# Where the tiles start in SBUF: small tiles ahead of and behind the large ones, large tiles at multiples of 2048 bytes

## The chip, the cores and the metric

One core of one Trainium2 chip runs the program. The metric is device time in microseconds (us) of one execution; the kernel before takes 1871.26 us (median of 3 runs, 1870.98 to 1871.41). Less is better.

## The reference

Two layers of a hybrid block on one sequence of 512 tokens with 1024 features. Each layer normalises `x`, projects it to 11 groups of features, and runs three branches: attention over 128 selected keys per query, a gated linear recurrence, and a chunked spatial gate. The branches are gated, merged, projected back and added to `x`; then a squared-ReLU FFN of width 4096 and a gated per-layer embedding are added in the same way. Cut to its products:

```
h = rms_norm(x, g_pre_mix);  proj = h @ w_in                      # 1024 -> 6216 features
y_a, y_b, y_c = attention(...), rg_lru(...) * gelu(gr), gating(...)
merged = einsum(sigmoid(gate_logits), einsum('nbsw,nwd->nbsd', stack(y_a, y_b, y_c), w_branch))
x = x + rms_norm(merged @ w_out, g_post_mix)
f = square(relu(rms_norm(x, g_pre_ffn) @ w_ffn_up)) @ w_ffn_down
x = x + rms_norm(f, g_post_ffn)
x = x + rms_norm((p_i @ w_ple) * sigmoid(x @ w_ple_gate), g_post_ple)
```

## The kernel before, in words

Activations lie transposed in SBUF, features on the 128 partitions and the 512 tokens along the free dimension, so one tile is 128x512 fp32: 2048 bytes in each partition. Every fp32 product is made of three fp32r products: each operand is split into a rounded high part and the rest (`split`, lines 359 to 365), and `mm3` (lines 289 to 292) issues high·high, weight-low·high and weight-high·low into the same PSUM bank. `gemm` (line 294) runs over 8 slices of 128 features: 24 matmuls of 512 columns for one output tile. `gemm_halves` does the same in halves of 256 columns where a norm has to start early, `gemm_arriving` (line 348) where the right-hand tiles are still being made, `tokens` (line 585) with the roles exchanged (activation slices are the weights of the array, the weight tile streams). Attention has its own small products (lines 651, 654, 923, 937).

Weights come from HBM in chunks of 128x1024 fp32 on SP's queue into three buffers `wr`; ScalarE makes the high part `wh` (line 235) and VectorE the low part `wl` (line 236), four buffers each, three chunks ahead of their use. The order of the chunks is written out in the list `order`. Work of the other branches (indexer, attention, recurrence) is slotted between matmuls by `tick`, which counts estimated microseconds on `clk`; the estimates are constants in the code, so the order of instructions does not depend on addresses.

What sets addresses: `cp`, `wp` and `tp` are pools; a tile of a new tag gets the next free bytes of its pool, in the order in which the tags first appear, and pools follow one another. A tile's size is rounded up to 32 bytes. The first free byte of a partition is 16512 (8·2048 + 128), behind constants of the program. In the kernel before, small tiles (`rt`, `sm`, `vec`, `m8`, `cnt`, `mx` and others) appear between large ones. The tiles start here, as the program is built before the change:

```
tile (first of a family)   start   mod 2048   mod 128   mod 64
X0 .. X7                   16512        128         0        0
ident (128x128 fp32)       32896        128         0        0
ropeC, ropeS, sacc         36128       1312        32       32
xh0, xl0 .. xh7, xl7       42400       1440        32       32
R                          75936        160        32       32
M4 .. M1, B0 .. B7         78240        416        32       32
A0 .. A7                  107168        672        32       32
V0, K0, K1, V1 (8192 B)   123552        672        32       32
M2                        156576        928        32       32
M3                        158752       1056        32       32
wr, wh, wl (4096 B)       161120       1376        96       32
tmp (11 of them)          206176       1376        96       32
```

So `xh`, `xl`, `A`, `B`, `K`, `V`, `M`, `tmp`, `wh`, `wl` and `sacc`, which are all the large operands of matmuls, start 32 bytes behind a multiple of 64, and a slice of 128 columns of them (512 bytes) does too. `X`, which no matmul reads, and `ident`, which the transposes stream, start at multiples of 64. Before `xh0` a tile `lead` of 128 bytes is allocated that nothing uses (line 464).

Of the kernel before, what the change touches and what calls it, by code (L numbers as in the profile page):

```python
# [8 lines left out]
F32 = mybir.dt.float32  # L9
F32R = mybir.dt.float32r  # L10
BF16 = mybir.dt.bfloat16
I32 = mybir.dt.int32
# [5 lines left out]
S = 512  # L18
D = 1024
KT = 8  # L20
# [22 lines left out]
NVEC = 76  # L43
# [7 lines left out]
def hybrid_block_kernel(ctx, tc, xT, pT, pos, vec, bsp, freq, w_in, w_tok, w_lru, w_sp, w_br, w_out, w_up, w_dn, w_ple, w_gate, out, depth=DEPTH, dbg=None):  # L51
# [3 lines left out]
    cp = ctx.enter_context(tc.tile_pool(name="cp", bufs=1))  # L55
    wp = ctx.enter_context(tc.tile_pool(name="wp", bufs=1))
    tp = ctx.enter_context(tc.tile_pool(name="tp", bufs=1))
    pp = ctx.enter_context(tc.tile_pool(name="pp", bufs=1, space=PSUM))

    uid = [0]  # L60

    def nm(p):
        uid[0] += 1
        return f"{p}_{uid[0]}"

    def tmp(dt=F32):
        return tp.tile([128, S], dt, tag="tmp", name=nm("tmp"), bufs=NTMP)

    def small(n, tag="sm", bufs=8):
        return cp.tile([128, n], F32, tag=tag, name=nm(tag), bufs=bufs)  # L70

    def bank():
        return pp.tile([128, 512], F32, tag="ps", name=nm("ps"), bufs=8)

    def slot(tag, dt=F32, big=False):
        return cp.tile([128, 4, S] if big else [128, S], dt, tag=tag, name=nm(tag))
# [8 lines left out]
    NWB = 4  # L85
    LAG = 1
    TAIL = 3
    ATT = 13
    WARM = 120
    FIRST = [0, 1, 4]  # L90


    X = [cp.tile([128, S], F32, tag=f"X{k}", name=f"X{k}") for k in range(KT)]
    ident = cp.tile([128, 128], F32, tag="ident", name="ident")
    make_identity(nc, ident)
    warm = cp.tile([128, 1], F32, tag="warm", name="warm")
    V.memset(warm, 0.0)
    A.activation(warm, warm, AF.Square)
    ones2 = cp.tile([128, 2], F32, tag="ones2", name="ones2")
    V.memset(ones2, 1.0)  # L100
    mhalf = cp.tile([128, 4], F32, tag="mhalf", name="mhalf")
    V.memset(mhalf, -0.5)
    BIAS = [cp.tile([128, 128 * (t + 1)], BF16, tag=f"bias{t}", name=f"bias{t}") for t in range(4)]

    V.memset(BIAS[3], 1.0)
    wps = bank()
    for _ in range(WARM):
        PE.matmul(wps[:, 0:64], BIAS[3][:, 0:128], BIAS[3][:, 0:64], start=True, stop=True)


    tri = BIAS[0]
    G.memset(tri, 0.0)
    G.affine_select(out=tri, in_=tri, compare_op=ALU.is_ge, fill=NEG, base=0, pattern=[[-1, 128]], channel_multiplier=1)
    fq = cp.tile([128, 8], F32, tag="fq", name="fq")
    posi = cp.tile([128, 4], I32, tag="posi", name="posi")

    ropeC = cp.tile([128, S], F32, tag="ropeC", name="ropeC")
    ropeS = cp.tile([128, S], F32, tag="ropeS", name="ropeS")

# [133 lines left out]
    def defer(us, fn):  # L253
        later.append((clk[0] + us, uid[0], fn))
        uid[0] += 1
# [8 lines left out]
    def add_task(q, gen):  # L264
        q["wait"].append(gen)
# [17 lines left out]
    def finish(q):  # L283
        run_later(force=True)
        while q["act"] or q["wait"]:
            tick(0.3)
# [39 lines left out]

    def gemm_arriving(keys, xs, source, ranges, arrived=None, lag=LAG, tail=TAIL):


        n = len(keys)  # L330
        ws = [getw(key, 0) for key in keys[:-1]]
        pss = [bank() for _ in keys]
        last = {}
        for r in ranges:
            gen = source(r)
            for k in range(KT):
                with ordered(last):
                    next(gen)
                    todo = [(o, k) for o in range(len(ws))]
                    if len(ws) < n and k == lag:  # L340
                        ws.append(getw(keys[-1], 0))
                        todo += [(n - 1, q) for q in range(k + 1)]
                    if r is ranges[-1] and k >= KT - tail:
                        todo = [] if k < KT - 1 else [(o, q) for o in range(n) for q in range(KT - tail, KT)]
                    for i, (o, q) in enumerate(todo):
                        h3, l3 = [v.rearrange("p (k c) -> p k c", k=KT) for v in ws[o]]
                        for m in range(3):
                            PE.matmul(pss[o][:, r], (h3, l3, h3)[m][:, q], xs[q][m // 2][:, r], start=q == 0 and m == 0, stop=q == KT - 1 and m == 2)  # L348
                        if r is ranges[-1] and q == KT - 1 and o < n - 1:
                            prep()  # L350
                tick(0.65 * len(todo) * width(r) / S)
            if arrived is not None:
                arrived(r)
        while nprep[0] < nget[0] + LA:
            prep()
        return pss
# [103 lines left out]
                tick(0.1)  # L460
            return self.gens[r.start]


    cp.tile([128, 32], F32, tag="lead", name="lead")
    XS = [(slot(f"xh{k}", F32R), slot(f"xl{k}", F32R)) for k in range(KT)]

    def x_tiles(r, xs, g=None, st=None, ys=None, bc=None, gp=None, on_g=()):
# [3 lines left out]
        def updated(d):  # L471
            if ys is not None and d < KT:
                if gp is None:
                    V.tensor_mul(ys[d][:, r], ys[d][:, r], bc)
                else:
                    V.scalar_tensor_tensor(ys[d][:, r], ys[d][:, r], gp[:, d:d + 1], bc, op0=ALU.mult, op1=ALU.mult)
                (G if d in on_g else V).tensor_add(X[d][:, r], X[d][:, r], ys[d][:, r])  # L477

        updated(0)
        for d in range(KT):  # L480
            x = X[d][:, r]
            if xs is not None:
# [14 lines left out]
                    V.scalar_tensor_tensor(lo, x, g[:, d:d + 1], f32v(hi), op0=ALU.mult, op1=ALU.subtract)  # L497
            yield d

    vecs = [cp.tile([128, NVEC], F32, tag=f"vec{l}", name=f"vec{l}") for l in range(depth)]  # L500
    nc.sync.dma_start(vecs[0], vec[0])
    nc.scalar.dma_start(posi, pos)
    nc.scalar.dma_start(fq, freq)
# [9 lines left out]
    for k in range(KT):  # L513
        if k in FIRST:
            c = slice(128 * k, 128 * (FIRST + [KT])[FIRST.index(k) + 1])
            for src, raw, hi, lo in chunks:
                nc.sync.dma_start(raw[:, c], src[:, c])
        nc.sync.dma_start(X[k], xT[k])

# [8 lines left out]
    for l in range(depth):  # L528
# [19 lines left out]
        rt = st.rt  # L548
        first = gemm_arriving([("in", l, f"xr{j}") for j in range(3)], XS, norm.source if l else lambda r: gen0, HALVES if l else (FULL,), st.row(D, R), 0, TAIL if l else 1)

        def proj(name, ahead=LA):
            ps = bank()
            gemm(ps, getw(("in", l, name), ahead), XS, KT)
            return ps
# [11 lines left out]
        def rope(ps, n=128):  # L566
            t1, u = tmp(), tmp()
            V.tensor_mul(t1[:n], ps[:n], Cr[:n])
            V.stream_shuffle(u[:n], ps[:n], mask=SHUF)
            G.tensor_mul(u[:n], u[:n], Sr[:n])  # L570
            G.tensor_add(t1[:n], t1[:n], u[:n])  # L571
            return t1
# [108 lines left out]
        def select(t, sc):  # L681
# [20 lines left out]
            G.tensor_add(gt[:, :n], gt[:, :n], eq[:, :n])  # L702
            G.tensor_scalar(BIAS[t], gt[:, :n], -NEG, NEG, op0=ALU.mult, op1=ALU.add)
            yield 1.0
# [47 lines left out]
        for j in range(4):  # L752
            mx = tmp()
# [49 lines left out]
        sp8 = small(4, "sp8", 2)  # L803
        V.tensor_scalar(sp8, h, 8.0, None, op0=ALU.mult)
        nsp8 = small(4, "nsp8", 2)
# [70 lines left out]
        def gated(n, ys, first=None, ds=range(8)):  # L876
            for d in ds:
                th = first if first is not None and d == 0 else gate(n, d)
                if d % 2 == 0:
                    w = getw(("br", l, n, d // 2), ahead=1)  # L880
                branch(n, d, w, ys, th)
# [10 lines left out]
        def attention(j):  # L892
# [6 lines left out]
            def logits(t):  # L899
                n = 128 * (t + 1)  # L900
                pr = qk(q2, kk, (ql, ql), kk, slice(t * 128, (t + 1) * 128), max(n, 256))
                for s in range(2):
# [5 lines left out]

                    V.tensor_tensor_reduce(lt, pr[s][:, :n], BIAS[t], scale=-ATT_SCALE, scalar=3.0e38, op0=ALU.add, op1=ALU.min, accum_out=mx[:, 0:1])
                    A.activation(lt, lt, AF.Exp, scale=-1.0, bias=mx[:, 0:1], accum_out=mx[:, 1:2])  # L910
# [82 lines left out]
        for j in range(4):  # L993
            f = rope(proj(f"q{j}"))
# [8 lines left out]
            if j == 0:  # L1003
                finish(idxq)
            defer(ATT, lambda j=j: add_task(attq, attention(j)))
            gated(1, YB, ds=range(2 * j, 2 * j + 2))
# [113 lines left out]
        gp = small(8, "gp", 2)  # L1120
# [12 lines left out]
    for r in HALVES:  # L1133
        for d in norm.source(r):
            (nc.sync if d % 2 == 0 else nc.scalar).dma_start(out[d, :, r], X[d][:, r])

# [76 lines left out]
```

## Time and profile before

| what | value |
|---|---|
| median of 3 runs | 1871.26 us |
| the profiled execution's own time | 1871.55 us |
| its span, first to last instruction | 1869.8 us |
| TensorE matmul busy | 1825.9 us (98%), 8798 instructions |
| TensorE weight load busy | 1503.1 us (80%) |
| VectorE / ScalarE / GpSimd busy | 1158.4 (62%) / 802.4 (43%) / 365.8 us (20%) |
| DMA | 167.77 MB, mean 90 GB/s |
| mean granted TensorE clock | 0.992 of full speed |

Matmuls are pipelined: the duration in a row (0.39 us for 512 columns) overlaps the next one's. What a matmul costs in a run of them is the distance of the starts. A row of a window counts each matmul that lies in it wholly or in part, so the distance is the window's length plus one duration, over the count.

### The profile page before, as it was taken

The page shows a single profiled execution, that of the slowest core. Times are in us where ns is not written, and L with a number is a line of the kernel's source. Part 1 is how long each engine was busy: PE and PEld are TensorE (multiplying, and loading weights), DVE is VectorE, ACT ScalarE, POOL GpSimd, SP SyncE. Part 2 cuts the span into 40 slices and gives each one's busy share as a digit, 9 for nine tenths or more (in the row PEclk, how much of TensorE's full clock was granted, in tenths as well). Part 3 has the DMA queues.
Part 4 walks back from the last instruction along what each step waited for, and adds up shares of the span by engine and source line. Part 5 has one row for each costly group of instructions (what it writes and reads, how often), then busy time and mean ns, then how long its engine had stood idle before and what let it go on. Part 6 is the DMA issues. An engine that isn't in the chain of part 4 may idle for free.

```text
span 1869.8 us, 22869 instructions
## 1 busy us (share of the span) xinstructions
PE 1825.9 (98%) x8798; PEld 1503.1 (80%) x8798; DVE 1158.4 (62%) x1939; ACT 802.4 (43%) x1292; POOL 365.8 (20%) x292
## 2 busy tenths in 40 slices
PE   8999999999999999999999999999999999999997
PEld 7678777788888888888886787887888888888886
DVE  6689976666286253533686999666563852535355
ACT  5466436564453222223444572455544432222233
POOL 3513222210240000003454141222003200000033
PEclk9999999999999999999999999999999999999998
DMA  5122222222223322332212222222222223232321
GB/s 171 62 91 84 97 91 91 68 80 79 86 84 104 100 93 99 95 109 90 91 58 95 69 90 99 94 80 69 90 79 91 91 90 102 92 100 92 111 79 57
DMA packets 49679, 167.77 MB, mean 90 GB/s; under 512 B 6049, under 2 KB 8865, under 8 KB 49569
## 3 DMA queue, kind: packets, MB, share of 16 engines
q1 hardware_dynamic: 47376, 163.64, 27.0%
q10 hardware_dynamic: 2192, 2.67, 0.5%
q8 instruction: 69, 1.13, 0.3%
q14 instruction: 42, 0.34, 0.1%
HBM read 164.19 MB, written 2.10 MB: 89 GB/s over the span
## 4 chain that ended last, share of the span: by engine, by line
PE 74%; DVE 11%; POOL 6%; issue 5%; ACT 4%; DMA 0%; SPq 0%; POOLq 0%; ACTq 0%; DVEq 0%
PE ps L290 21%; PE ps L292 20%; PE ps L291 20%; PE ps L348 4%; PE ps L585 4%; DVE tmp L689 2%; DVE wl L236 2%; DVE m L687 2%; POOL tmp L570 1%; POOL tmp L571 1%; PE ps L937 1%; PE ps L654 1%; PE ps L651 1%; POOL sacc L390 1%; POOL X L477 1%
## 5 line engine op out<-in xcount | busy, mean ns | idle before, releaser
L235 ACT CAST wh<-wr 128x1024 fp32r<-128x1024 f32 x303 | 317.0, 1049 | 468.7 <-PE ps L292 382.8
L236 DVE TENSOR_TENSOR wl<-wr,wh 128x1024 fp32r<-128x1024 f32 x303 | 386.2, 1278 | 201.8 <-ACT wh L235 201.7
L290 PE MATMUL ps<-xh,wh 128*128 128x512 f32 (+1 forms) x1296 | 506.9, 391 | 0.0
L292 PE MATMUL ps<-xl,wh 128*128 128x512 f32 (+1 forms) x1296 | 498.1, 384 | 0.0
L291 PE MATMUL ps<-xh,wl 128*128 128x512 f32 (+1 forms) x1296 | 495.7, 382 | 0.8 <-DVE wl L236 0.8
L390 POOL TENSOR_TENSOR sacc<-sacc,tmp 128x256 f32<-128x256 f32 (+1 forms) x99 | 110.3, 1115 | 902.9 <-issue 590.1
L292 PEld LDWEIGHTS ps<-xl,wh 128*128 128x128 f32 x1296 | 243.4, 188 | 50.1
L290 PEld LDWEIGHTS ps<-xh,wh 128*128 128x128 f32 x1296 | 243.7, 188 | 49.4 <-issue 4.9
L291 PEld LDWEIGHTS ps<-xh,wl 128*128 128x128 f32 x1296 | 243.7, 188 | 46.9 <-DVE wl L236 1.7
L292 PE MATMUL ps<-V,wh 128*128 128x512 f32 (+1 forms) x528 | 196.8, 373 | 0.0
L290 PE MATMUL ps<-K,wh 128*128 128x512 f32 (+1 forms) x432 | 159.9, 370 | 0.0
L291 PE MATMUL ps<-K,wl 128*128 128x512 f32 (+1 forms) x432 | 157.9, 366 | 0.0
L292 PE MATMUL ps<-B,wh 128*128 128x512 f32 x336 | 131.9, 392 | 0.0
L290 PE MATMUL ps<-A,wh 128*128 128x512 f32 x320 | 126.6, 396 | 0.0
L291 PE MATMUL ps<-A,wl 128*128 128x512 f32 x320 | 124.8, 390 | 0.0
L1072 DVE TENSOR_TENSOR M<-M,ps 128x512 f32<-128x512 f32 x48 | 33.1, 689 | 143.8 <-PE ps L292 143.8
L292 PEld LDWEIGHTS ps<-V,wh 128*128 128x128 f32 x528 | 99.3, 188 | 18.5
L1060 DVE TENSOR_TENSOR tmp<-ps,R 128x512 f32<-128x512 f32 x64 | 43.8, 689 | 111.5 <-PE ps L292 111.5
L348 PE MATMUL ps<-xl,wh 128*128 128x256 f32 (+1 forms) x264 | 88.4, 335 | 7.8 <-DVE xl L497 7.2
L291 PEld LDWEIGHTS ps<-K,wl 128*128 128x128 f32 x432 | 81.2, 188 | 14.3
L290 PEld LDWEIGHTS ps<-K,wh 128*128 128x128 f32 x432 | 81.3, 188 | 13.2
L348 PE MATMUL ps<-xh,wh 128*128 128x256 f32 (+1 forms) x264 | 87.1, 330 | 0.5 <-ACT xh L487 0.5
(239 smaller groups left out, 2745.5 us busy)
## 6 DMA issues: line engine op xcount, KB each, us to landing
wr<-in_w_in_dram SPq DMA_DIRECT2D x95, 512.0 KB, 3.3
wr<-in_w_up_dram SPq DMA_DIRECT2D x64, 512.0 KB, 3.3
wr<-in_w_dn_dram SPq DMA_DIRECT2D x64, 512.0 KB, 3.3
wr<-in_w_br_dram SPq DMA_DIRECT2D x24, 512.0 KB, 3.3
wr<-in_w_tok_dram SPq DMA_DIRECT2D x16, 512.0 KB, 3.3
wr<-in_w_out_dram SPq DMA_DIRECT2D x16, 512.0 KB, 3.3
wr<-in_w_gate_dram SPq DMA_DIRECT2D x16, 512.0 KB, 3.3
X<-in_xT_dram SPq DMA_DIRECT2D x8, 256.0 KB, 5.8
```

The source lines that it names most:

```text
L235: A.copy(hi, raw)
L236: V.tensor_sub(lo, raw, f32v(hi))
L290: PE.matmul(ps, wh, xh, start=start, stop=False)
L291: PE.matmul(ps, wl, xh, start=False, stop=False)
L292: PE.matmul(ps, wh, xl, start=False, stop=stop)
L348: PE.matmul(pss[o][:, r], (h3, l3, h3)[m][:, q], xs[q][m // 2][:, r], start=q == 0 and m == 0, stop=q == KT - 1 and m == 2)
L390: G.tensor_add(sacc[:, r], sacc[:, r], self.q[r.start, r.stop])
L585: PE.matmul(ps, x, w, start=k == 0 and i == 0, stop=k == KT - 1 and i == 2)
L687: V.max(m8, (sc if r == 0 else wk)[:, :n])
L689: V.match_replace(wk[:, :n], m8, (sc if r == 0 else wk)[:, :n], -3.0e38)
L1060: V.tensor_mul(t, ps, R)
L1072: V.tensor_add(F[d], F[d], ps)
```

## The change

All allocations of small tiles are made ahead of the first large tile, in `cp` (one unused allocation of each small tag, so that its buffers lie there; `vec0`; `warm` becomes a buffer of the tag `sm`), or in a new pool `ep` behind `tp` (`ident`, `ones2`, `mhalf`, the biases, `fq`, `posi`, `vec1`). Then a tile `lead` of 256 bytes fills up to the next multiple of 2048; the old one of 128 bytes goes. The small tiles take 1344 bytes and `vec0` 320; with `lead` that is 1920, and 16512 + 1920 = 18432 = 9·2048. From there on `cp` holds only tiles of 2048 and 8192 bytes, `wp` of 4096 and `tp` of 2048. No instruction is added or removed, and no size, buffer count, order or queue is changed.

```diff
+    ep = ctx.enter_context(tc.tile_pool(name="ep", bufs=1))
     pp = ctx.enter_context(tc.tile_pool(name="pp", bufs=1, space=PSUM))
...
+    LEAD = 256
...
-    X = [cp.tile([128, S], F32, tag=f"X{k}", name=f"X{k}") for k in range(KT)]
-    ident = cp.tile([128, 128], F32, tag="ident", name="ident")
+
+    for n, tag, bufs in ((4, "sm", 8), (4, "rt", 4), (32, "wi", 2), (8, "m8", 4), (1, "cnt", 4), (4, "sp8", 2), (4, "nsp8", 2), (2, "mx", 8), (8, "gp", 2)):
+        small(n, tag, bufs)
+    vecs = [(ep if l else cp).tile([128, NVEC], F32, tag=f"vec{l}", name=f"vec{l}") for l in range(depth)]
+    ident = ep.tile([128, 128], F32, tag="ident", name="ident")
     make_identity(nc, ident)
-    warm = cp.tile([128, 1], F32, tag="warm", name="warm")
+    warm = small(1)
     V.memset(warm, 0.0)
     A.activation(warm, warm, AF.Square)
-    ones2 = cp.tile([128, 2], F32, tag="ones2", name="ones2")
+    ones2 = ep.tile([128, 2], F32, tag="ones2", name="ones2")
     V.memset(ones2, 1.0)
-    mhalf = cp.tile([128, 4], F32, tag="mhalf", name="mhalf")
+    mhalf = ep.tile([128, 4], F32, tag="mhalf", name="mhalf")
     V.memset(mhalf, -0.5)
-    BIAS = [cp.tile([128, 128 * (t + 1)], BF16, tag=f"bias{t}", name=f"bias{t}") for t in range(4)]
+    BIAS = [ep.tile([128, 128 * (t + 1)], BF16, tag=f"bias{t}", name=f"bias{t}") for t in range(4)]
...
-    fq = cp.tile([128, 8], F32, tag="fq", name="fq")
-    posi = cp.tile([128, 4], I32, tag="posi", name="posi")
-
+    fq = ep.tile([128, 8], F32, tag="fq", name="fq")
+    posi = ep.tile([128, 4], I32, tag="posi", name="posi")
+
+    cp.tile([128, LEAD // 4], F32, tag="lead", name="lead")
+    X = [cp.tile([128, S], F32, tag=f"X{k}", name=f"X{k}") for k in range(KT)]
     ropeC = cp.tile([128, S], F32, tag="ropeC", name="ropeC")
...
-
-    cp.tile([128, 32], F32, tag="lead", name="lead")
     XS = [(slot(f"xh{k}", F32R), slot(f"xl{k}", F32R)) for k in range(KT)]
...
-    vecs = [cp.tile([128, NVEC], F32, tag=f"vec{l}", name=f"vec{l}") for l in range(depth)]
     nc.sync.dma_start(vecs[0], vec[0])
```

## Rows read from the trace of the kernel before

**Rows 1.** The page: busy time by engine, and TensorE's granted clock in 40 slices.

```profile
PE 1825.9 (98%) x8798; PEld 1503.1 (80%) x8798; DVE 1158.4 (62%) x1939; ACT 802.4 (43%) x1292; POOL 365.8 (20%) x292
...
PEclk9999999999999999999999999999999999999998
```

**Rows 2.** The waits of TensorE: waiting line, releaser, total us, times, longest.

```profile
PE ps L348 <- DVE xl L497: 7.2, 9, 3.8
PE ps L651 <- DVE A L638: 7.1, 8, 1.9
PE ps L585 <- DVE wl L236: 4.1, 2, 2.1
```

**Rows 3.** Windows, TensorE alone: stretch, length, busy us (matmuls), granted clock, DMA.

```profile
600.00:860.00 260.00, 260.00 (x1137) 1.00 0.31 98
...
451.00:496.00 45.00, 45.00 (x195) 1.00 0.28 90
...
497.20:507.20 10.00, 10.00 (x87) 1.00 0.22 75
...
241.00:256.00 15.00, 15.00 (x66) 1.00 0.42 138
...
512.50:514.50 2.00, 2.00 (x20) 1.00 0.72 221
```

**Rows 4.** Timeline, TensorE: start us, duration us, line, tiles, shape, count.

```profile
660.72 0.39 PE L291 MATMUL ps<-xh,wl 128*128 128x512 f32 x1
...
662.09 0.39 PE L291 MATMUL ps<-xh,wl 128*128 128x512 f32 x1
...
451.20 0.40 PE L291 MATMUL ps<-A,wl 128*128 128x512 f32 x1
...
452.60 0.40 PE L291 MATMUL ps<-A,wl 128*128 128x512 f32 x1
...
512.55 0.28 PE L292 MATMUL ps<-V,wh 128*128 128x256 f32 x1
...
513.23 0.28 PE L292 MATMUL ps<-V,wh 128*128 128x256 f32 x1
```

**Rows 5.** Timeline, TensorE: transposes, and products with two columns.

```profile
31.94 1.03 PE L155 MATMUL ps<-ident,tmp 128*128 128x128 f32 x8
...
35.56 0.95 PE L400 MATMUL ps<-ones,sacc 128*128 128x2 f32 x8
```

**Rows 6.** Matmuls grouped by line and shape: count, busy us, mean ns, idle before.

```profile
L290 PE MATMUL ps<-xh,wh 128*128 128x512 f32 x1200 | 479.8, 400 | 0.0
...
L348 PE MATMUL ps<-xl,wh 128*128 128x256 f32 x176 | 52.4, 298 | 4.0 <-DVE xl L497 3.5
...
L155 PE MATMUL ps<-ident,tmp 128*128 128x128 f32 x8 | 1.0, 272 | 0.0
```

**Rows 7.** Casts of ScalarE grouped by line and shape, columns as in the group before.

```profile
L361 ACT CAST A<-tmp 128x512 fp32r<-128x512 f32 x32 | 19.9, 622 | 11.8 <-DVE tmp L1061 11.8
...
L485 ACT CAST xh<-X 128x512 fp32r<-128x512 f32 x16 | 9.8, 623 | 18.9 <-POOL X L477 16.3 <-DVE X L477 2.6
```

**Rows 8.** DMA issues: tiles, queue, count, size, median us to landing.

```profile
wr<-in_w_in_dram SPq DMA_DIRECT2D x95, 512.0 KB, 3.3
...
X<-in_xT_dram SPq DMA_DIRECT2D x8, 256.0 KB, 5.8
```

**Rows 9.** Windows, all engines: PE, PEld, DVE, ACT, POOL busy us (instructions), clock, DMA.

```profile
140.00:235.00 95.00, 93.09 (x412) 75.96 (x411) 93.14 (x168) 51.24 (x64) 30.61 (x22) 1.00 0.28 89
1065.00:1165.00 100.00, 96.00 (x420) 77.92 (x419) 98.09 (x177) 52.80 (x65) 30.61 (x22) 1.00 0.26 85
```

## The prediction

> **What bounds the kernel now.** I read the busy shares first: TensorE is busy 1825.9 of 1869.8 us and its clock is granted at the full 2.4 GHz level in nearly every slice [rows 1]. The reader is to see that there is almost no idle time to win. The waits of TensorE say the same: the three largest come to 18.4 us [rows 2]. An edit that adds and removes no instruction can then move the time only through what one matmul costs, so the third view is the distance of matmul starts in stretches without a wait, by windows.
>
> From 600 to 860 us, pure 512-column products: (260 + 0.39) / 1137 = 229.0 ns [rows 3]. 512 columns at 2.4 GHz are 213.3 ns, so 15.7 ns of each matmul, 6.9%, are not columns. From 451 to 496 us it is more: six starts take 452.60 - 451.20 = 1.40 us, 233.3 ns each [rows 4], and the window agrees, (45 + 0.40) / 195 = 232.8. The operands there are `A`, then `K` and `V`; the same `K` and `V` slots stream at the 229 ns pace later (their products lie inside 600 to 860 us). The token products of line 585 have 233.3 ns too: (15 + 0.40) / 66 [rows 3]. With 256 columns (106.7 ns at 2.4 GHz) two paces occur: (10 + 0.28) / 87 = 118.2 ns, and 0.68 / 6 = 113.3 ns [rows 3, 4].
>
> These paces are not arbitrary. 16 columns of fp32 are 64 bytes in a partition and take 16 / 2.4 = 6.67 ns. In that unit the paces are 233.3 = 35.0, 113.3 = 17.0, 229.0 = 34.35, 118.2 = 17.7. So 512 columns, 32 units, take 34.33 (103 units for three matmuls) or 35; 256 columns, 16 units, take 17 or 17.7. A stream that costs whole units of 64 bytes, always at least one too many, is what I would expect if operands are fetched in pieces of 64 bytes and every operand starts in the middle of one: 2048 bytes that begin 32 bytes behind a multiple of 64 touch 33 pieces, 1024 bytes touch 17. That is how all large matmul operands lie before the change, and the unit is an inference from the paces, not something a row states.
>
> **The change part by part.** Small tiles and `vec` move: no instruction, DMA or queue order changes, so their cost is zero on both sides. `warm` becomes a buffer of the ring `sm`: the eighth allocation after it has to wait for a ScalarE Square issued at the start of the program, over 30 us earlier; nothing. The unused allocations have no reader or writer to wait for.
>
> The large tiles of ScalarE and VectorE operands: a cast whose source is `X`, at a multiple of 64 before the change, takes 623 ns, and one whose source is `tmp`, 32 bytes off, takes 622 ns [rows 7]. Reading at a multiple of 64 gains nothing there. No row shows a write of either at such a place except VectorE's and GpSimd's into `X`, which compete with one another; and both engines are hidden behind TensorE, so I take 0. Weight transfers land in 3.3 us, and each is issued three chunks ahead, some 16 us at 5.5 us a chunk; faster or slower by 10% is hidden. The first load of `X` lands in 5.8 us [rows 8] and lies on the path once: within 0.5 us either way, taken as 0.
>
> The matmul operands: 6,808 matmuls have 512 columns (24 groups of the listing by shape) and 1,424 have 256 (17 groups); [rows 6] shows the largest group of each. The trace holds no fp32r matmul whose moving operand starts at a multiple of 64, so the new pace is bounded from both sides. Below: the transposes stream `ident`, which did start at a multiple of 64. Eight of them, first start to last end, take 1.03 us and one lasts 0.272 us [rows 5, 6], so seven starts take 0.758 us, 108.3 ns each: if they need two clocks for each of 128 columns, that is 106.7 + 1.6 ns, with no unit of 6.67 ns on top. At that excess, call it 2 ns, a 512-column matmul would cost 215.3 ns, 13.7 less than now. Above: 233.3 ns, the slower pace that exists already, 4.3 more than now. Between them I take the nearest to what the rows count: one unit of 64 bytes fewer, the same hand-over behind it, so 33.33 units, 222.2 ns, 6.7 less.
>
> Sum: 6,808 x 6.67 ns = 45.4 us. For 256 columns one unit less would be 111 ns, but there the weight load is the next limit: eight products of only two columns take 0.95 us to the last end with 0.24 for one, 0.1 us each [rows 5], and 113.3 ns is the best pace seen. So 1,424 x (118.2 - 113.3) = 7.0 us at most; many of these stand in stretches that wait for a norm (the group with 176 has a mean of 298 ns against a streaming duration of 280), and I take half, 3.5. What is late next: in two stretches VectorE is busy 93.1 of 95 and 98.1 of 100 us [rows 9]. There the 412 + 420 matmuls can't go faster than VectorE's work lets them; I take their 832 x 6.67 = 5.5 us as lost to new waits. Elsewhere VectorE and ScalarE have a third of their time or more to spare. Together 45.4 + 3.5 - 5.5 = 43.4 us. Span 1869.8 - 43.4 = 1826.4; 1.75 us lie around the span in the profiled execution (1871.55), which stands 0.3 us above the median of the runs: 1826.4 + 1.75 - 0.3 = 1828 us.
>
> [...]
>
> **The rivals.** (a) *The whole excess goes.* If the straddled start delays every piece of the stream rather than adding one, a matmul falls to 215.3 ns. For: the excess grows with the columns (6.6 or 11.5 ns at 256, 15.7 or 20 at 512), and a fixed extra piece would not. Against: 512 columns never run at 33 units now, so part of the excess is something else. Time: 6,808 x 13.7 = 93.3, plus 3.5, less 832 x 13.7 = 11.4 in VectorE's stretches: -85.4, 1786 us.
>
> (b) *Nothing changes.* The excess is the stream's own: 17/16 of 213.3 is 226.7 and of 106.7 is 113.3, and both numbers are there; fp32r would simply run 17 clocks for 16 columns wherever it starts. For: proportional excess, and ScalarE's indifference to the start [rows 7]. Against: the transposes show none. Time 1871 us. That the change does not do what it says falls here too, but 16512 + 1920 is 9·2048, and every later size is a multiple of 2048, so I give it nothing.
>
> (c) *Slower.* The pace of 35 units takes over everywhere. It lasts for 45 us at a time with operands that stream at 34.33 elsewhere, so it is a way of locking and not a property of one tile; and in the token products, where the moving operand is `wh` (96 bytes behind a multiple of 128) and the array's weights come from `xh` (32 behind), it is always there. Which lock is reached seems to hang on how the moving stream and the weight load stand to one another, and with every tile at the same phase they start in the same place each time. It decides once the 34.33 pace is no longer reached after a wait. 384 token products and some 390 in the two slow stretches pay it already: (6,808 - 774) x 4.3 ns = 26 us, 1897 us.
>
> **How the numbers follow.** Forecast 0.35, (a) 0.22, (b) 0.25, (c) 0.18. A change of 0.2%, 3.7 us, is about what these runs can tell from none. Forecast and (a) are faster: 0.57; (b) the same: 0.25; (c) slower: 0.18. The forecast's own range is 1815 to 1845 (the 256-column and VectorE terms both ways, and 33 to 34 units); (a) reaches down to 1775; on the other side the range takes in (b) with its neighbours up to 1885 and leaves most of (c) out.
>
> **What would show it.** In a stretch like 600 to 860 us: 222 ns if the forecast is right, 215 for (a), 229 for (b), 233.3 for (c); the paces in units of 6.67 ns would show whether one piece went. VectorE's and ScalarE's casts should keep 622 ns, the transposes about 108 ns. The stretches with VectorE at 95% or more should show new waits of TensorE on VectorE. The prediction is wrong if the 512-column pace stays within 1 ns of 229.0, or if it falls and the span does not follow because waits grow by as much.

## The result, and the profile after

The changed kernel takes 1861.01 us (median of 4 runs, 1858.04 to 1864.48); the kernel before takes 1871.34 us beside it (4 runs, 1870.98 to 1872.86). The ratio is 0.9942, 95% interval 0.9925 to 0.9959: about 10 us faster, where the prediction said 43. The profiled execution of the changed kernel has a span of 1857.0 us (1858.77 us with what lies around it), 12.8 us less than the span before.

The page after: span, busy time by engine and TensorE's granted clock, answering to [rows 1].

```profile
span 1857.0 us, 22869 instructions
...
PE 1812.3 (98%) x8798; PEld 1502.8 (81%) x8798; DVE 1158.3 (62%) x1939; ACT 801.9 (43%) x1292; POOL 365.0 (20%) x292
...
PEclk9999999999999999999999999999999999999999
```

TensorE's busy time falls by 13.6 us with the same 8,798 instructions and a granted clock of 0.993 after 0.992; no other engine changes by 1 us. The waits of TensorE after (columns as in [rows 2]; the lines have moved, L348 is L355, L651 is L655, L585 is L589 and L291 is L298) come to 36 us in all where they came to 35; those on `wl` grow, the one on L298 from the 3.8 us of L291, a line of before shown last:

```profile
PE ps L355 <- DVE xl L502: 7.1, 9, 3.8
PE ps L655 <- DVE A L642: 6.7, 10, 1.2
PE ps L589 <- DVE wl L243: 5.0, 2, 2.5
PE ps L298 <- DVE wl L243: 4.6, 4, 1.7
...
PE ps L291 <- DVE wl L236: 3.8, 4, 1.5
```

So the time went where the prediction looked for it, into the distance of matmul starts. Windows after, TensorE alone, columns as in [rows 3]; the second is the stretch of `A`, `K` and `V` that stood at 451 to 496 us before:

```profile
600.00:860.00 260.00, 260.00 (x1149) 1.00 0.29 99
...
449.00:494.00 45.00, 45.00 (x201) 1.00 0.29 94
...
241.00:256.00 15.00, 15.00 (x68) 1.00 0.38 125
```

From 600 to 860 us (260 + 0.39) / 1149 = 226.6 ns against 229.0. In the `A`, `K`, `V` stretch (45 + 0.40) / 201 = 225.9 against 232.8 (a little too low, for the last three of the 201 have 256 columns), in a window of nearly all token products (15 + 0.40) / 68 = 226.5 against 233.3. Single starts show a sharper value. The timeline after, TensorE, columns as in [rows 4], two rows of each of three stretches:

```profile
450.45 0.39 PE L298 MATMUL ps<-A,wl 128*128 128x512 f32 x1
...
451.81 0.39 PE L298 MATMUL ps<-A,wl 128*128 128x512 f32 x1
...
500.33 0.28 PE L298 MATMUL ps<-K,wl 128*128 128x256 f32 x1
...
501.77 0.28 PE L298 MATMUL ps<-K,wl 128*128 128x256 f32 x1
...
655.07 0.39 PE L298 MATMUL ps<-xh,wl 128*128 128x512 f32 x1
...
656.43 0.39 PE L298 MATMUL ps<-xh,wl 128*128 128x512 f32 x1
```

Six starts of 512 columns take 1.36 us in both places, 226.7 ns: 34.0 units of 6.67 ns. Twelve starts of 256 columns take 1.44 us, 120.0 ns: 18.0 units, *more* than the 113.3 to 118.2 ns before [rows 3, 4]. The 256 columns between the two cost 106.7 ns, 0.417 ns each. That is the 2.4 columns a nanosecond which the prediction writes as 2.4 GHz, and on it rest its unit of 6.67 ns, 16 columns, and its 213.3 ns for 512.

Over the whole trace, taking each start and the next of the same width, and of these distances the ones of 180 to 240 ns at 512 columns and 90 to 130 at 256 (longer ones are waits, first starts after a wait or after other products, or the lower clock): 6,407 distances at 512 columns had a mean of 229.56 ns before and have 227.29 after (6,405 of them), 1,141 at 256 columns had 116.83 and have 119.57 (1,152). 6,407 x 2.27 = 14.5 us gained, 1,141 x 2.74 = 3.1 us lost, 11.4 us together, of the span's 12.8. The mean lies above 226.7 because of the first products after a start, which vary as in the bursts of experiment 5: after the change the first ten distances of each unbroken row of them have a mean of 229.96 ns (1,218 of them), the rest 226.67 (5,187).

The two stretches with a busy VectorE, all engines, columns as in [rows 9]:

```profile
140.00:235.00 95.00, 92.70 (x409) 76.14 (x408) 93.14 (x169) 51.03 (x63) 30.56 (x22) 1.00 0.27 89
1065.00:1165.00 100.00, 95.24 (x418) 77.86 (x418) 97.97 (x179) 51.51 (x66) 27.95 (x20) 1.00 0.29 95
```

VectorE is as busy as before, and nearly as many matmuls fit in. Taking the same matmul in both traces, its start comes 1.22 us earlier after than before at 140 us and 1.66 us at 235; 7.15 us at 1065 and 7.33 us at 1165: these stretches gain 0.44 and 0.18 us. From 600 to 860 us the lead grows from 3.70 to 6.22 us.

Casts of ScalarE, one transpose group of TensorE, and the loads after (columns as in [rows 7], [rows 5] and [rows 8]):

```profile
L368 ACT CAST A<-tmp 128x512 fp32r<-128x512 f32 x32 | 19.9, 623 | 11.9 <-DVE tmp L1065 11.9
...
L490 ACT CAST xh<-X 128x512 fp32r<-128x512 f32 x16 | 9.8, 624 | 18.9 <-POOL X L482 16.3 <-DVE X L482 2.6
```

```profile
31.04 1.04 PE L162 MATMUL ps<-ident,tmp 128*128 128x128 f32 x8
```

```profile
wr<-in_w_in_dram SPq DMA_DIRECT2D x95, 512.0 KB, 3.3
...
X<-in_xT_dram SPq DMA_DIRECT2D x8, 256.0 KB, 5.7
```

All as before within 1 ns, 0.01 us and 0.1 us: these casts, transposes and transfers took as long at the new starts.

### The profile page after: what moved, and what is told of

Its sections match the earlier page's. It is cut to its first block, busy times and chain, and to the rows that moved or that the text cites. A ratio compares the mean times of both kernels' runs of the same rounds, so it can differ in the third digit from the quotient of the medians.

```text
span 1857.0 us, 22869 instructions
## 1 busy us (share of the span) xinstructions
PE 1812.3 (98%) x8798; PEld 1502.8 (81%) x8798; DVE 1158.3 (62%) x1939; ACT 801.9 (43%) x1292; POOL 365.0 (20%) x292
## 4 chain that ended last, share of the span: by engine, by line
PE 73%; DVE 12%; POOL 6%; issue 4%; ACT 4%; DMA 0%; SPq 0%; POOLq 0%; ACTq 0%; DVEq 0%
PE ps L297 21%; PE ps L299 20%; PE ps L298 20%; PE ps L355 3%; PE ps L589 3%; DVE tmp L693 2%; DVE wl L243 2%; DVE m L691 2%; POOL tmp L574 1%; POOL tmp L575 1%; PE ps L941 1%; PE ps L658 1%; POOL sacc L397 1%; POOL X L482 1%; PE ps L655 1%
## 5 line engine op out<-in xcount | busy, mean ns | idle before, releaser
L298 PE MATMUL ps<-xh,wl 128*128 128x512 f32 (+1 forms) x1296 | 495.0, 382 | 1.2 <-DVE wl L243 1.2
L298 PEld LDWEIGHTS ps<-xh,wl 128*128 128x128 f32 x1296 | 244.1, 188 | 44.4 <-DVE wl L243 2.0
L298 PE MATMUL ps<-K,wl 128*128 128x512 f32 (+1 forms) x432 | 157.8, 365 | 0.0
L298 PE MATMUL ps<-A,wl 128*128 128x512 f32 x320 | 124.5, 389 | 0.0
L355 PE MATMUL ps<-xl,wh 128*128 128x256 f32 (+1 forms) x264 | 87.9, 333 | 7.8 <-DVE xl L502 7.1
L298 PEld LDWEIGHTS ps<-K,wl 128*128 128x128 f32 x432 | 81.5, 189 | 13.1
L355 PE MATMUL ps<-xh,wh 128*128 128x256 f32 (+1 forms) x264 | 86.2, 327 | 1.2 <-ACT xh L492 1.2
```

The source lines that it names most:

```text
L298: PE.matmul(ps, wl, xh, start=False, stop=False)
```

## The experiments

What was open: is it the start of each operand (at a multiple of 64, or of 2048), is it the small tiles, or is it how two operands stand to one another? For the last, call the *difference* the start of the weights (the operand loaded into the array) less the start of the moving operand, in bytes of the partition. Starts modulo 2048 before: `xh` and `xl` 1440, `A`, `K`, `V` 672, `B` and `M` 416, `wr`, `wh`, `wl` and `tmp` 1376. After: all 0.

**1. Operands at a multiple of 64 in the kernel before.**

```diff
-    cp.tile([128, 32], F32, tag="lead", name="lead")
+    cp.tile([128, 40], F32, tag="lead", name="lead")
```

> The kernel before with its unused tile ahead of xh0 made 160 bytes instead of 128: every matmul operand from xh0 on moves from 32 to 0 modulo 64, and the tiles stay at mixed places modulo 2048 (xh at 1472, M and B at 448, A, K and V at 704, weights and tmp at 1408). Theory 64 (only the place within 64 bytes counts): the paces of the changed kernel, 226.7 ns at 512 columns and 120.0 at 256, and 1860 us. Theory 2048 (a tile must not cross a multiple of 2048): 229 and 233 ns as before, 1871 us. Theory phase (all tiles must stand alike): moving and weight tiles differ by 64 bytes modulo 128 as before, so 229 ns and 1871 us.

Measured: 1871.29 us (12 runs, 1868.76 to 1873.57), ratio 1.0007, interval 0.9998 to 1.0015. Windows, TensorE alone:

```profile
600.00:860.00 260.00, 260.00 (x1138) 1.00 0.30 99
...
241.00:256.00 15.00, 15.00 (x66) 1.00 0.32 103
```

1138 matmuls against 1137 before, 66 token products against 66. Every operand starts at a multiple of 64 and nothing has changed: the prediction's cause, a straddled piece of 64 bytes, falls. All starts moved together, so the differences are those of before.

**2. and 3. The changed kernel with its large tiles off the multiple of 2048, by 32 and by 64 bytes.**

```diff
-    LEAD = 256
+    LEAD = 32
```

That is run 2, with all large tiles at 1824 modulo 2048; run 3 has `LEAD = 64`, with all at 1856.

> The changed kernel with a filler of 32 bytes instead of 256: every large tile lies at 1824 modulo 2048, which is 32 modulo 64, and all stand alike. Theory 64: the gain is gone, paces 229 and 233 ns at 512 columns and 117.8 at 256, 1871 us. Theory phase: the paces of the changed kernel stay, 226.7 and 120.0 ns, 1861 us. Theory 2048: gone, 1871 us.

> The changed kernel with a filler of 64 bytes: every large tile lies at 1856 modulo 2048, which is 64 modulo 128 and 0 modulo 64, all alike. Theory 64 and theory phase: 226.7 and 120.0 ns, 1861 us. Theory 2048 (or any unit above 64 bytes): 229 ns or more, 1871 us.

Measured: 1859.59 us (6 runs), ratio 0.9945, interval 0.9933 to 0.9957; and 1862.88 us (5 runs), ratio 0.9961, interval 0.9949 to 0.9973. Both keep the changed kernel's paces (means of 227.3 ns at 512 and 119.6 at 256 columns). The window of run 2:

```profile
600.00:860.00 260.00, 260.00 (x1149) 1.00 0.30 99
```

1149 matmuls with tiles 32 bytes off a multiple of 64, as many as with tiles at multiples of 2048. The multiple is not what counts; that all tiles stand alike may be.

**4. The changed kernel with the weights alone 32 bytes on.**

```diff
     XS = [(slot(f"xh{k}", F32R), slot(f"xl{k}", F32R)) for k in range(KT)]
+    wp.tile([128, 8], F32, tag="wlead", name="wlead")
```

> The changed kernel with 32 unused bytes ahead of the weight pool: wr, wh, wl and tmp lie at 32 modulo 2048, the activations stay at multiples of 2048. In gemm the array's weights are off and the moving operand is not; in the token products it is the other way round. Theory 64 for the moving operand alone: 226.7 ns in gemm, 233 ns in the token products (384 matmuls, 2.5 us), 1863 us. If the weight load's place counts: 229 ns in gemm, 1871 us.

Measured: 1891.03 us (4 runs, 1889.74 to 1891.33), ratio 1.0111, interval 1.0098 to 1.0124. One unused tile of 32 bytes makes the kernel 30 us slower than the changed one. The page's busy time, and the window:

```profile
PE 1849.0 (98%) x8798; PEld 1502.7 (80%) x8798; DVE 1158.0 (61%) x1939; ACT 803.0 (43%) x1292; POOL 364.8 (19%) x292
```

```profile
600.00:860.00 260.00, 260.00 (x1116) 1.00 0.30 97
```

(260 + 0.40) / 1116 = 233.3 ns: 35 units at 512 columns, now throughout (the mean over the trace is 233.23). The moving operands are where the changed kernel has them. In run 2 both operands were 32 bytes off and the gain stayed; here the weights alone are, and it turns into a loss. So it is the relation between the two operands. Neither theory of the expectation named this time: they had 1863 and 1871 us.

**5. The difference by itself: a probe.** It leaves the kernel's computation out; its core is

```python
for i in range(48):                       # one burst, no wait inside; the bursts follow one another
    k, m = i // 3 % 8, i % 3              # hi x hi, lo weights x hi, hi weights x lo, over 8 slices
    PE.matmul(ps[:, :n], st[:, w:w + 128], mv[:, x:x + n], ...)   # w - x set by the difference
```

> A probe, not the block: it leaves out the whole computation and runs bursts of 48 matmuls, 24 in gemm's order twice, on fp32r data that nothing else touches. The moving operand starts at a multiple of 512 bytes, the weights of the array d bytes behind one, d from 0 to 512 (and 4, 8, 16, 48), three bursts of each d at 512 columns, two at 256. Then both are shifted by 32, then the moving operand alone by 32 and 64, then bfloat16. Theory phase modulo 128: 34.0 units of 6.67 ns (226.7 ns) at d = 0, 128, 256, 384, 512; 34.33 or 35 at 64, 192, 320, 448; 35 at 32, 96 and the like; shifting both by 32 changes nothing. Rival, the relation counts over a larger span: d = 128 or 256 differ from d = 0. Rival, traffic of the other engines makes the excess: without it all d have one pace, under 34 units. At 256 columns: 18.0 units at d = 0, 17.67 at 64, 17.7 at 32. bfloat16 at 512 columns, half the bytes: within 4 ns of 213.3 ns if the excess comes from the bytes that the two streams fetch.

The timeline of the probe, TensorE, one row per burst of 48: start us, us from its first start to its last end, tile names, shape. In the first fence, 512 columns, the differences are 0, 32, 64, 192 and 256 from the top, and the last row has bfloat16 operands; in the second, 256 columns, 0 and 64. In brackets stands the idle time before the burst. Each of the three probes was executed once.

```profile
38.01 11.20 PE L75 MATMUL ps<-mv,st 128*128 128x512 f32 x48 [0.73 <-ACT res L76]
49.94 11.47 PE L75 MATMUL ps<-mv,st 128*128 128x512 f32 x48 [0.73 <-ACT res L76]
62.14 11.47 PE L75 MATMUL ps<-mv,st 128*128 128x512 f32 x48 [0.73 <-ACT res L76]
...
110.93 11.26 PE L75 MATMUL ps<-mv,st 128*128 128x512 f32 x48 [0.73 <-ACT res L76]
...
135.10 11.20 PE L75 MATMUL ps<-mv,st 128*128 128x512 f32 x48 [0.73 <-ACT res L76]
...
1045.74 10.52 PE L92 MATMUL ps<-b 128*128 128x512 bf16 x47 [0.73 <-ACT res L76]
```

```profile
692.32 6.00 PE L75 MATMUL ps<-mv,st 128*128 128x256 f32 x48 [0.73 <-ACT res L76]
...
705.31 5.93 PE L75 MATMUL ps<-mv,st 128*128 128x256 f32 x48 [0.52 <-ACT res L76]
```

A burst of 512 columns starts slowly (its first distance is 333 to 344 ns, and the next ten or so can vary) and then settles on a pace that repeats within 0.1 ns in every repetition in this probe. The mean of the last 24 distances of each burst, ns:

```
difference      0     4     8    16    32    64    96   128   160   192   224   256   288   320   384   448   512
512 columns 226.7 232.3 230.7 233.3 233.3 233.3 234.3 232.7 233.3 228.9 233.3 226.7 233.3 233.3 232.1 228.9 226.7
256 columns 120.0 118.3 115.5 118.3 118.3 117.8 118.6 118.8 120.0 117.8 117.8 120.0 118.3 117.8 118.5 113.3 120.0
```

At 512 columns the pace repeats with 256 bytes but for 0.6 ns at 128 and 384. The expectation's theory, a repeat with 128 bytes, falls (128 is 6 ns slower than 0), and so does its rival that traffic of other engines makes the excess: there is next to none here (a DMA share of 0.00 or 0.01 in the windows of this probe, and one ScalarE copy between bursts). At 256 columns 192 and 448 gave 117.8 and 113.3 here, and 117.8 both in the second probe, where other bursts went before: the difference alone does not fix the pace of a burst; whether it also hangs on how the burst starts was not shown. With both operands moved by 32 bytes, difference 0 still gives 226.7 ns, and 32 and 64 still give 233.3; with the moving operand alone moved by 32 and 64 bytes, which is a difference of 224 and 192 modulo 256, the paces are 233.3 and 228.9 as in the table. Now the kernels can be read off. Before, the weights stand -64, 704 or 960 bytes behind `xh`, `A` and `B`: 192 modulo 256 each time, 228.9 ns; in the token products, with the roles exchanged, 64: 233.3 ns. Run 1 has the same differences. The changed kernel and runs 2 and 3 have 0 everywhere: 226.7 and 120.0. Run 4 has 32: 233.3 and 118.3.

**6. The whole gain from 64 bytes in the kernel before.** No small tile and no activation moves; only `wr`, `wh`, `wl` and `tmp` do.

```diff
     XS = [(slot(f"xh{k}", F32R), slot(f"xl{k}", F32R)) for k in range(KT)]
+    wp.tile([128, 16], F32, tag="wlead", name="wlead")
```

> The kernel before with one unused tile of 64 bytes ahead of the weight slots: small tiles, vec, ident and all activation slots stay where they were; only wr, wh, wl and tmp move up by 64 bytes. The weights then start 0, 768 or 1024 bytes behind the moving operands, that is 0 modulo 256, while no large tile lies at a multiple of 64. Theory (the pace hangs on the difference of the weights' start and the moving operand's start, modulo 256, and on nothing else of the change): 512 columns at 226.7 ns, 256 columns at 120 ns, token products 226.7 ns, and the whole gain of the change, 1860 to 1863 us. Rival (the multiple of 2048, or the place of the small tiles, carries part of the gain): 1866 us or more. Rival of the prediction (a start at a multiple of 64 bytes is what counts): 1871 us.

Measured: 1862.11 us (5 runs, 1860.42 to 1864.05), ratio 0.9944, interval 0.9931 to 0.9958: the same as the change. Windows, TensorE alone:

```profile
600.00:860.00 260.00, 260.00 (x1149) 1.00 0.30 98
...
241.00:256.00 15.00, 15.00 (x68) 1.00 0.38 126
```

1149 and 68, the counts of the changed kernel. The theory gave 1860 to 1863 us.

**7. The whole change but for the difference.**

```diff
-    LEAD = 256
+    LEAD = 64
...
+    wp.tile([128, 48], F32, tag="wlead", name="wlead")
```

> The kernel after with a leading tile of 64 bytes instead of 256 and an unused tile of 192 bytes ahead of the weight slots: every matmul operand starts at a multiple of 64, weights at multiples of 2048 and activations 192 bytes lower modulo 256. Theory (difference modulo 256): the paces of the kernel before, 228.9 ns at 512 columns, 233.3 ns in the token products (difference 64 there), about 117.8 ns at 256 columns; 1869 to 1873 us. Rivals (alignment to 64 or 2048, or the moved small tiles, count): at or near 1861 us.

Measured: 1872.29 us (11 runs, 1869.47 to 1873.71), ratio 1.0000, interval 0.9991 to 1.0009. The window:

```profile
600.00:860.00 260.00, 260.00 (x1137) 1.00 0.30 98
```

1137, the count of before; its mean distances (229.51 ns at 512 columns, 117.22 at 256, 233.3 in the token products) are those of before too. With the small tiles moved and the large ones at multiples of 64, but the weights 192 on, nothing is left of the gain.

**8. A difference of 256.**

```diff
-    LEAD = 256
+    LEAD = 32
...
+    wp.tile([128, 64], F32, tag="wlead", name="wlead")
```

> The kernel after with a leading tile of 32 bytes and an unused tile of 256 bytes ahead of the weight slots: activations at 1824, weights at 32 modulo 2048, difference 256. Theory (modulo 256): as the changed kernel, 226.7 and 120 ns, 1859 to 1864 us. Rival (operands must start alike modulo 2048): another pace, and 1870 us or more.

Measured: 1862.12 us (5 runs), ratio 0.9941, interval 0.9929 to 0.9954, with 1148 matmuls from 600 to 860 us. Operands that start alike modulo 256, and not modulo 2048, have the whole gain.

**9. Where the excess comes from: fewer weight columns, and alternating differences.** A second probe, again without the kernel's computation.

> Probe; the kernel's computation is left out. Bursts of 48 products that follow one another without a wait, with new weights in each product. Part 1: weights start 0, 448, 464, 480, 496, 504, 508, 192, 208, 240, 248, 64 bytes behind the moving operand, at 512 and 256 columns. Part 2: only 64 or 32 weight columns, differences 0, 32, 64, 192. Part 3: the difference alternates between 0 and 32, 64 or 192 from product to product, once by the weights and once by the moving operand. Theory 1 (the excess over 213.3 ns comes from the weight load reading beside the moving stream): with 64 columns of weights the excess over 213.3 ns halves, to about 220 ns at difference 0, and falls again with 32. Rival (the excess is the moving stream's own, and the weights only shift its phase): the paces stay as with 128 columns. In part 3, if the load of the next weights beside the present stream decides, the alternating bursts take a pace between those of the two differences, about 230 ns with 32; if one bad start in any product sets a lasting lock, 233.3 ns.

The timeline, one row per burst of 48: 64 weight columns with difference 0 and 32, then 128 columns with the moving operand going to and fro by 64 bytes, so that the difference alternates between 64 and 0.

```profile
482.85 11.26 PE L75 MATMUL ps<-mv,st 128*64 128x512 f32 x48 [0.52 <-ACT res L76]
494.83 11.34 PE L75 MATMUL ps<-mv,st 128*64 128x512 f32 x48 [0.72 <-ACT res L76]
...
712.39 11.18 PE L75 MATMUL ps<-mv,st 128*128 128x512 f32 x48 [0.73 <-ACT res L76]
```

With 64 columns the settled paces are 230.0 ns at difference 0, 231.7 at 32, 232.8 at 64 and 228.3 at 192; with 32 columns 231.7, 240.0, 231.7 and 231.7. Half the weights do not halve the excess over 213.3 ns; at difference 0 it grows from 13.3 to 16.7 ns. Theory 1 of the expectation, that the excess is the time in which the weight load reads beside the stream, falls; its rival, that the paces stay, is off by up to 6.7 ns. Alternating bursts gave 226.7 to 235.0 ns and decide nothing: neither theory's value holds throughout, and with the weights alternating between 0 and 32 the same burst settled at 235.0 ns in one repetition and at 230.0 in the other, so at 512 columns too one burst can settle on two paces. Part 1 found no difference below 226.7 ns at 512 columns (464 bytes: 232.0; 480: 233.3; 496: 228.3; 504 and 508: 233.3).

**10. Columns, rows, types.** A third probe, without the kernel's computation.

> Probe; the kernel's computation is left out. Bursts of 48 gapless products, new weights in each. Part 1: 512, 480, 448, 384, 320, 256 columns, with the weights 0, 32 and 192 bytes behind the moving operand. At difference 0 the earlier probe had 34 units of 6.67 ns for 512 columns and 18 for 256, that is columns/16 + 2. Theory A (at difference 0 a product pays a fixed hand-over of 13.3 ns): 32, 30, 26 and 22 units for 480, 448, 384 and 320 columns, 213.3, 200.0, 173.3 and 146.7 ns. Theory B (the stream itself is slower, in proportion): between them the excess over columns/2.4 shrinks with the columns. Part 2 at 512 columns: the same weights in every product, the same moving operand, both, and 64 rows in place of 128. If the excess is interference of this product's stream with the next one's weight load, fixed weights change nothing as long as they are loaded again, 226.7 ns at difference 0. Part 3: bfloat16 operands, the weights 0, 32, 64, 96, 128 and 192 bytes from a multiple of 256: 215.8 ns in all if only fp32r operands have this dependence; a spread of several ns if it holds for both.

The timeline, one row per burst of 48: 480 columns with difference 0 and 32; 384 with 0, 32 and 192; bfloat16 at 512 with the weights 64 bytes off a multiple of 256.

```profile
74.88 10.67 PE L75 MATMUL ps<-mv,st 128*128 128x480 f32 x48 [0.73 <-ACT res L76]
86.25 10.82 PE L75 MATMUL ps<-mv,st 128*128 128x480 f32 x48 [0.70 <-ACT res L76]
...
141.20 8.60 PE L75 MATMUL ps<-mv,st 128*128 128x384 f32 x48 [0.68 <-ACT res L76]
150.42 8.60 PE L75 MATMUL ps<-mv,st 128*128 128x384 f32 x48 [0.62 <-ACT res L76]
159.64 8.59 PE L75 MATMUL ps<-mv,st 128*128 128x384 f32 x48 [0.62 <-ACT res L76]
...
723.50 10.52 PE L81 MATMUL ps<-b 128*128 128x512 bf16 x48 [0.73 <-ACT res L82]
```

Settled paces at differences 0, 32, 192: 480 columns 216.7, 220.0, 218.3 ns; 448 columns 202.8, 204.5, 200.0; 384 columns 173.3 in all three; 320 columns 146.7 in all three; 256 columns 120.0, 118.3, 117.8. Theory A (a fixed 13.3 ns at difference 0) holds at 512, 384, 320 and 256 and misses at 480 and 448 by 3.4 and 2.8 ns; Theory B falls. At 384 and 320 columns the pace is the same at all three. The same weights or the same moving operand in every product change nothing (226.7 at difference 0). bfloat16 has 215.8 ns at every one of six starts: of the two types tried, the dependence belongs to fp32r alone.

## Why the prediction was wrong, point by point

**What bounds the kernel: right.** Busy time of TensorE fell by 13.6 us with its waits within 1 us of before, and the span followed.

**The small tiles, the casts, the loads at nothing: right.** Experiments 6 and 7 bracket them: the gain comes whole without moving a small tile (1862.11 us), and with all of them moved and the difference kept it is 0 (1872.29 us). VectorE's and GpSimd's additions into `X` do compete, as the prediction says: in the trace of before VectorE's of 128x512 take 0.69 us where GpSimd is idle (four of them) and 1.01 us where GpSimd adds beside them (two).

**The step that failed** is "one unit of 64 bytes fewer, the same hand-over behind it, so 33.33 units, 222.2 ns, 6.7 less", with the sentence under it that "operands are fetched in pieces of 64 bytes and every operand starts in the middle of one". No run shows such pieces. Experiment 1 puts every operand at a multiple of 64 and gains nothing (1871.29 us); experiment 2 has no operand there and gains everything (1859.59 us). What the change did was to make the difference 0 where it had been 192 (64 in the token products). That is worth 228.9 - 226.7 = 2.2 ns in most products, and 6.6 in those that had run at 35 units, the token products and the `A`, `K`, `V` stretch (of which more under what stays open). The term of 45.4 us came out as 14.5. That the time moved the way that was forecast is luck: tiles at multiples of 2048 also stand alike, and where the differences were kept (experiments 1 and 7) nothing was gained.

Part of the evidence was there. The token products used the very tiles of `gemm` with the roles exchanged and were slower, 233.3 against 229.0 ns, though each operand's own start was 32 bytes off a multiple of 64 in both uses. A cause in the start of one operand can't tell these apart; a cause in the pair can. (The two paces of the `K` and `V` slots are no such evidence: their difference is 192 in both places.) The prediction said as much in rival (c), "how the moving stream and the weight load stand to one another", and priced it for the wrong case: it had equal starts as the way into 35 units, and at 512 columns none of the 26 differences tried was faster than equal starts, at 226.7 ns.

**The 256-column term** was taken as 3.5 us gained and came out as 3.1 lost: at difference 0 these products settle at 120.0 ns, the top of the table in experiment 5.

**VectorE's stretches: right in kind.** 832 products would have gained 832 x 2.27 = 1.9 us; 0.62 us came, so two thirds were lost there, where the prediction had all of its larger gain lost. They went into the waits that it named: the waits for `wl`, which VectorE makes, grew from 3.8 to 4.6 us on one line and from 4.1 to 5.0 on the other, and all four of the one and one of the two of the other lie in these stretches.

**The rivals.** (a), 215.3 ns: not for fp32r; no probe came under 226.7 at 512 columns. (b): its proportional 17/16 named 226.7 for 512 columns but 113.3 for 256, where 120.0 was measured, and experiment 10 shows the excess over 0.417 ns a column to be 13.3 ns at difference 0 with 256, 320, 384 and 512 columns alike. (c): 35 units everywhere do exist, and experiment 4 reaches it with 32 bytes; it costs 1891.03 - 1870.57 (the kernel before beside it) = 20.5 us where (c) had 26. Of the 6,407 x 3.67 = 23.5 us at 512 columns and 1.5 at 256, TensorE's waits gave some 5 back: they sum to 35 us before and to 30 in run 4.

**What stays open** is why the difference counts. Theory 1 of experiment 9 was one guess, but fewer weight columns should then have helped, and they hardly did: with 64 in place of 128 the pace is 3.3 ns slower at difference 0 and 0.5 to 1.6 ns faster at 32, 64 and 192. No run here separates the two reads. Nor is it settled why `A`, `K` and `V` ran at 35 units from 451 to 496 us before, at a difference of 192 that gave 228.9 ns in every burst of the probes. But the runs show that the difference does not decide it. Windows inside that stretch, TensorE alone: of before, of run 1, and of run 7 in the first layer and in the second, with a difference of 192 in each.

```profile
453.00:494.00 41.00, 41.00 (x177) 1.00 0.28 91
...
452.00:493.00 41.00, 41.00 (x181) 1.00 0.29 91
...
454.00:495.00 41.00, 41.00 (x181) 1.00 0.28 91
1379.00:1420.00 41.00, 41.00 (x177) 1.00 0.28 90
```

177 matmuls in 41 us is the pace of 233.3 ns, 181 that of 228.9. Run 1 has the faster pace, and run 7 has it in one layer and not in the other. So at a difference of 192 this stretch can settle on either pace; whether that hangs on how the stretch starts was not tried by itself. With some 390 products in the two layers and 233.3 - 228.9 = 4.4 ns each, an estimated 1.7 us of what the change gained may come from this and not from 228.9 going to 226.7.

## What to carry to other kernels

Where fp32r products follow one another without a wait, look at the starts of the two operands in the partition: with the weights' start less the moving operand's start at a multiple of 256 bytes, 512-column products ran at 226.7 ns, with many others at 233.3 (at 384 and 320 columns the three differences tried were alike, 173.3 and 146.7 ns, and at 256 columns equal starts, 120.0 ns, were among the slowest); one unused tile between the activations and the weights cost one version of this kernel 30 us (32 bytes) and gave another 10 (64 bytes). Every edit of the allocations can change that difference by accident, so print the starts before putting a few tenths of a per cent down to anything else. And when a cost shows a dependence on place, ask of the rows whether one operand can explain it: a pair that is slower with its roles exchanged says that it can't.

## What the runs showed of the hardware that was not expected

The excess of fp32r products over their columns is gone at the lower clock. In three of six bursts with 64 rows the granted clock fell within the burst to 0.50, and it stayed there into the 128-row burst behind. Windows of the third probe, TensorE alone: the start of such a burst of 64 rows, its rest, the start of the 128-row burst behind it, and that burst's later part.

```profile
421.00:423.00 2.00, 2.00 (x9) 1.00 0.00 0
424.00:440.00 16.00, 15.85 (x38) 0.50 0.01 1
...
440.60:443.00 2.40, 2.40 (x6) 0.50 0.00 0
...
444.00:452.00 8.00, 8.00 (x36) 1.00 0.00 0
```

At 0.50 the distance of starts is 426.7 ns, at differences 0, 32 and 192, with 64 and with 128 rows: 0.833 ns a column, twice the 0.417 at the full clock. If a column takes twice as long at half the clock, nothing is left of the 13 to 20 ns; a fixed number of TensorE's clocks for each product would have doubled them.
